# Hand-written orders in a two-layer encoder kernel: first norm, x updates, last norm, third gate operand, and the place of the Fourier constants

## Chip, cores and metric

The kernel runs on one core of a Trainium2 chip. The metric is the device time of one execution in microseconds (us). An execution was also profiled; its span goes from the first to the last instruction of the program.

## What is computed

The input x is 512 tokens by 1024 channels in float32. Two layers of

```
x += 1/2 * SwiGLU(RMSNorm(x))                       # FFN 1
h  = RMSNorm(x)
x += W_o( sigmoid(ga) * NA(h) W_na + sigmoid(gf) * FNet(h) W_f )   # mixer; ga, gf are projections of h plus a bias
x += 1/2 * SwiGLU(RMSNorm(x))                       # FFN 2
```

and a last RMSNorm with a gain. NA is attention over a neighbourhood in an 8 x 64 grid of tokens with a learned bias by relative position; FNet is the real part of a 2-D Fourier transform over positions and the channels of a group. The inner width of an FFN is 2816.

## The kernel before

**Precision and products.** Every float32 operand is split into a high part (a copy on ACT, rounded to the format that PE takes) and a low part (operand minus high part, on DVE); line 285 is the helper, lines 287 and 288 its two instructions. A product is three matmuls (lines 281 to 283): high x high, high x low, low x high. Large products go through a seven-product scheme of Strassen's kind: of the four quarters of a weight and of an activation, sums and differences are made, and products 1 to 7 are added with signs. The weights for it arrive as quarters ("raw", 512 KB) through SP's queue (line 150); some differences are made by an accumulating load on POOL's queue (line 152, line 179), others by an add on DVE (line 170). `Item.prep` (line 164) splits one piece into `whi` (line 172 where it is negated, else 287) and `wlo` (173 or 288); three buffers hold each.

**Order.** The weights form one stream (`ws`): `ws.next()` hands out the next piece and first prepares two pieces further, and each preparation asks for loads up to eight pieces further (FETCH, line 33). A scheduler places the instructions of each engine by priority, which is the place in the program text except under `tc.high_priority()`; where the text says `tc.manual_schedule`, the engines named keep the order of the text. Engines run their instructions strictly in the order so made, each with its waits. PE is TensorE, DVE VectorE, ACT ScalarE, POOL GpSimd, SP the engine that issues most loads.

**First norm.** x comes twice at the start: transposed (`xt`, scaled and split at once in `given`, line 330) and by tokens (`x`, loaded at line 1251 behind eight weight pieces). The 1/rms of a token is applied late: `norm.rstd` (line 389) sums the squares (ACT with an accumulator, line 323, two per block of 128 tokens) and forms 1/sqrt by an integer start and three Newton steps, some 15 tiny operations on DVE (lines 299 to 304, 395 to 408). For the first norm it runs in the middle of the first products; `plain_out` (line 540) then needs it for the first 256 columns of the FFN: a tanh on ACT (line 545) and two operations on DVE (549, 550) for each block, and the transposes of their result (line 486) are the next work of PE after the third product of the first round.

**Updates in an FFN.** The products of the second matrix are added to x with signs by `update` (line 590, 128x512 each). After the last piece of product 6 three updates of two instructions each follow at once (line 680), then those of products 7, 3 and 4. The next norm's squares and transposes of x (`quad`) stand between them.

**Last norm.** In the last FFN the tokens of the second half are ready first: `finish` (line 718) makes 1/rms for them, one pass of 128x1024 for each block of 128 tokens, and stores them. `begin_block` (706) multiplies half of the channels of the other two blocks by the gain beforehand; `finish_block` (711) takes 1/rms for one block (`inverse`, line 372, a chain of twelve tiny operations under high priority), scales one half of the channels on ACT and the other on DVE, and stores them by ACT's and SP's queues. The last product goes block by block, so that block 0 ends 12 matmuls ahead of block 1.

**Mixer.** `stage_mixer` (line 729) loads the Fourier matrices (four loads of 256 KB on POOL's queue, line 747) and rotation constants (SP, 749) at its start, projects U, forms 1/rms and spreads it over the partitions through memory (`spread`, 410: a store and a broadcast load into `R`, both on POOL's queue), projects V, does the transform over positions (`four_pos`, 832, first user of the constants) and over channels, and attention with its bias (POOL, 893). Then come the gates: `gate_block` runs the seven products in the order 1, 5, 2, 6, 7, 3, 4. Its combined operands are made by hand at lines 1145 to 1152: t1 (for product 5) and t2 (for product 6) with ACT and DVE in the order of the text, and t3 (for product 7) by `third`, called after product 1.

Of the kernel before, what the change touches and what calls it, by code (L numbers as in the profile page):

```python
# [9 lines left out]
F32 = mybir.dt.float32  # L10
# [7 lines left out]
P = 128  # L18
# [74 lines left out]
def encoder_kernel(  # L93
# [213 lines left out]
    class Norm:  # L307


        def __init__(self, idx):  # L310
            self.idx = idx
            self.mix = idx % 3 == 1
            self.ssq = small("ssq")
            self.raw = {}
            self.due = []
            self.h = [None, None]
            self.l = [None, None]
# [54 lines left out]
        def inverse(self, tb):  # L372

            a, b = self.ssq[:, tb : tb + 1], self.ssq[:, 4 + tb : 5 + tb]
            e, f = small("e", 1), small("ef", 1)
            with tc.high_priority():
                V.tensor_scalar(e, a, 1.0 / D, EPS, ALU.mult, ALU.add)
                V.tensor_scalar(f, e, -0.5, None, ALU.mult)
                ms, mh, r, t = small("ms", 1), small("mh", 1), small("r", 1), small("rt", 1)
                V.tensor_scalar(ms, b, 1.0 / D, e, ALU.mult, ALU.add)  # L380
                V.tensor_scalar(mh, b, -0.5 / D, f, ALU.mult, ALU.add)
                V.tensor_single_scalar(t.bitcast(I32), ms.bitcast(I32), 1, ALU.logical_shift_right)
                V.tensor_scalar(r.bitcast(I32), t.bitcast(I32), -1.0, float(0x5F3759DF), ALU.mult, ALU.add)
                for _ in range(3):
                    V.tensor_scalar(t, r, r, mh, ALU.mult, ALU.mult)
                    V.tensor_scalar(r, t, 1.5, r, ALU.add, ALU.mult)
            return r

        def rstd(self, js=(0, 1)):
# [3 lines left out]
            ms = small("ms", n)  # L393
            with tc.high_priority():
# [75 lines left out]
    def stage_ffn(norm, nxt, late):  # L470
# [62 lines left out]
        late_at = []  # L533
        if not norm.idx:
            for i in range(2):
                for j in range(2):
                    norm.squares(i, j)
            norm.rstd()

        def plain_out():  # L540
# [69 lines left out]

        for jb in range(NB):
            f0 = 2 + 4 * jb
            pa = pair("A")
            product(pa, acts[1], K4, True)
            s1 = snap(pa)
            if jb:
                settle_at()
            pb = pair("B")
            product(pb, acts[5], K4, True)
            sb = snap(pb)  # L620
            if jb == 0 and norm.idx == 0:
                plain_out()
            else:
                settle_at()
            product(pa, acts[6], K4, False, again=True)
# [20 lines left out]
        for i, (m, c, _) in enumerate(steps):  # L646
# [16 lines left out]
            if not late:  # L663
                if i == 6:
                    nxt.quad(0, 0)
                elif m == 4 and c == 0:
                    nxt.quad(1, 1)
                    nxt.quad(0, 1)
            if c < 2:
                continue  # L670
            if m == 1:
                update(ps[1], 0, 0, -1)
            elif m == 2:
                update(ps[2], 0, 0, 1)
                nxt.squares(0, 0)
            elif m == 5:
                update(ps[5], 0, 1, 1)
                update(ps[5], 1, 1, -1)
            elif m == 6:
                for q in ((1, 1, 1), (0, 1, -1), (1, 0, 1)):  # L680
                    update(ps[1], *q)
            elif m == 7:
                update(ps[7], 1, 1, 1)
                nxt.squares(1, 1)
            elif m == 3:
                update(ps[3], 0, 1, 1)
                nxt.squares(0, 1)
                if late:
                    make(i + 3)
                    finish(nxt, 1)  # L690
                    for b in range(2):
                        begin_block(b)
            elif late:
                for b in range(2):
# [10 lines left out]

    def begin_block(tb):

        ob[tb] = slot(F32, "o", (D,))
        V.tensor_tensor(ob[tb][:, 0:T], x[:, tb, 0:T], gf[0][:, 0:T], ALU.mult)

    def finish_block(norm, tb):
        r, o_ = norm.inverse(tb), ob[tb]
        S.activation(o_[:, 0:T], o_[:, 0:T], AF.Copy, scale=r)
        S.dma_start(out=out[:, tb, 0:T], in_=o_[:, 0:T])
        V.scalar_tensor_tensor(o_[:, T:D], x[:, tb, T:D], r, gf[0][:, T:D], ALU.mult, ALU.mult)
        nc.sync.dma_start(out=out[:, tb, T:D], in_=o_[:, T:D])

# [11 lines left out]
    def stage_mixer(l, norm, nxt):  # L729
# [11 lines left out]
        nc.sync.dma_start(out=msk, in_=mask)  # L741
        dfs = [hilo("dft") for _ in range(2)]
        rt = slot(F32, "rot", (2, T))
        rots = [rt[:, 0, :], rt[:, 1, :]]
        for hl in range(2):
            for c in range(2):
                G.dma_start(out=dfs[c][hl], in_=dft[hl, c])
            src = bass.AP(tensor=rot.tensor, offset=rot.offset + hl * T, ap=[[0, P], [1, T]])
            nc.sync.dma_start(out=rots[hl], in_=src)

# [19 lines left out]
        def proj_U():  # L770
# [27 lines left out]
            norm.rstd()  # L798
            norm.spread(R)
            outs = []  # L800
            for c in range(2):
# [336 lines left out]
        def minus(p, q, s):  # L1138
            t, u = slot(F32, s), slot(F32, s)
            for z, d in enumerate((t, u)):  # L1140
                V.tensor_tensor(d, p[z], q[z], ALU.subtract)
            V.tensor_tensor(t, t, u, ALU.add)
            return t

        with tc.manual_schedule(engines={mybir.EngineType.DVE, mybir.EngineType.Activation}):
            ws.prep(ws.pos + 3)
            t12 = minus(B[0, 0], B[0, 1], "t1")
            acts[5] = parts(t12, "t1")
            for z in B[1, 1]:
                V.tensor_tensor(t12, t12, z, ALU.add)  # L1150
# [5 lines left out]
        def third():  # L1156
            acts[7] = parts(minus(B[0, 1], B[1, 1], "t3"), "t3")

# [4 lines left out]

        ga0 = gate_block(0, bias, acts, {1: third, 6: fourth})

# [76 lines left out]
    with tc.manual_schedule(engines={mybir.EngineType.SP}):  # L1242
        for kts in ((0,), (1,), (2, 3), (4, 5), (6, 7)):
# [147 lines left out]
```

## Time and profile before

| | us |
|---|---|
| three runs | 1950.65, 1950.5, 1947.32 (median 1950.5) |
| profiled execution | 1946.62 |
| its span | 1944.8 |
| PE busy | 1913.3 (98%) |
| DVE busy | 1617.2 (83%) |
| ACT busy | 1121.6 (58%) |
| mean granted TensorE clock | 0.997 |

Busy time is the union of an engine's instructions. Matmuls are pipelined: a 128x512 one is shown with about 0.39 us and the next starts after 0.227. A line of a timeline gives the start, the duration, the engine, the line of the kernel, the operation, out<-in, the form, how many were merged, and in brackets the idle time of the engine before it with what ended that. `LDWEIGHTS` and matmuls of PE are separate rows. "PEclk" is the granted clock as a share of the full one.

### The profile page before, as it was taken

The page shows a single profiled execution, that of the slowest core. Times are in us where ns is not written, and L with a number is a line of the kernel's source. Part 1 is how long each engine was busy: PE and PEld are TensorE (multiplying, and loading weights), DVE is VectorE, ACT ScalarE, POOL GpSimd, SP SyncE. Part 2 cuts the span into 40 slices and gives each one's busy share as a digit, 9 for nine tenths or more (in the row PEclk, how much of TensorE's full clock was granted, in tenths as well). Part 3 has the DMA queues.
Part 4 walks back from the last instruction along what each step waited for, and adds up shares of the span by engine and source line. Part 5 has one row for each costly group of instructions (what it writes and reads, how often), then busy time and mean ns, then how long its engine had stood idle before and what let it go on. Part 6 is the DMA issues. An engine that isn't in the chain of part 4 may idle for free.

```text
span 1944.8 us, 24572 instructions
## 1 busy us (share of the span) xinstructions
PE 1913.3 (98%) x8997; PEld 1582.6 (81%) x8997; DVE 1617.2 (83%) x1949; ACT 1121.6 (58%) x1596; POOL 198.7 (10%) x242
## 2 busy tenths in 40 slices
PE   8999999999999999999999999999999999999997
PEld 6888887888788888888788888878887888888885
DVE  8777899598789877889977878995978888787898
ACT  6555665346556655566655556653565566555654
POOL 0001011200111010001000100102111110000010
PEclk9999999999999999999999999999999999999999
DMA  9677499221997477649747765983029974766593
GB/s 314 165 195 201 151 248 325 80 72 44 256 232 204 131 190 207 177 156 261 233 139 198 198 174 164 276 277 102 31 87 255 240 185 131 210 181 173 173 281 125
DMA packets 105417, 361.83 MB, mean 186 GB/s; under 512 B 11984, under 2 KB 14160, under 8 KB 105296
## 3 DMA queue, kind: packets, MB, share of 16 engines
q1 hardware_dynamic: 77856, 266.37, 39.0%
q0 software_dynamic: 27008, 93.34, 26.2%
q8 instruction: 71, 1.16, 0.2%
q10 hardware_dynamic: 432, 0.55, 0.1%
q14 instruction: 50, 0.41, 0.1%
HBM read 354.97 MB, written 2.10 MB: 184 GB/s over the span
## 4 chain that ended last, share of the span: by engine, by line
PE 78%; DVE 13%; DMA 4%; issue 3%; ACT 2%; SPq 0%; POOL 0%; ACTq 0%; DVEq 0%; POOLq 0%
PE A L281 8%; PE A L283 8%; PE A L282 8%; PE B L283 4%; PE B L281 4%; PE o L282 4%; PE B L282 4%; PE o L283 4%; PE o L281 4%; PE ps L282 4%; PE ps L281 4%; PE ps L283 4%; DVE wlo L288 4%; DMA raw<-in_wst_dram 3%; PE C L282 2%
## 5 line engine op out<-in xcount | busy, mean ns | idle before, releaser
L288 DVE TENSOR_TENSOR wlo<-raw,whi 128x1024 fp32r<-128x1024 f32 (+1 forms) x522 | 620.2, 1194 | 258.4 <-ACT whi L287 256.1
L287 ACT ACTIVATE whi<-raw 128x1024 fp32r<-128x1024 f32 (+1 forms) x522 | 540.2, 1038 | 508.3 <-PE A L283 131.3
L152 POOL DMA_DIRECT2D raw<-in_wst_dram x152 | 131.2, 874 | 1341.2 <-DMA raw<-in_wst_dram 542.6
L170 DVE TENSOR_TENSOR raw<-raw,raw 128x1024 f32<-128x1024 f32 (+1 forms) x128 | 150.9, 1189 | 2.4
L282 PE MATMUL A<-wlo,xh 128*128 128x512 f32 x384 | 149.6, 390 | 1.4 <-DVE wlo L173 1.4
L283 PE MATMUL A<-whi,xl 128*128 128x512 f32 x384 | 149.5, 389 | 0.0
L281 PE MATMUL A<-whi,xh 128*128 128x512 f32 x384 | 149.3, 390 | 0.0
L172 ACT ACTIVATE whi<-raw 128x1024 fp32r<-128x1024 f32 x76 | 78.9, 1039 | 71.4 <-PE B L283 33.2
L173 DVE SCALAR_TENSOR_TENSOR wlo<-raw,whi 128x1024 fp32r<-128x1024 f32 x76 | 89.9, 1194 | 13.4 <-ACT whi L172 13.4
L282 PEld LDWEIGHTS A<-wlo,xh 128*128 128x128 f32 x384 | 72.1, 188 | 17.3 <-DVE wlo L173 2.3
L281 PEld LDWEIGHTS A<-whi,xh 128*128 128x128 f32 x384 | 71.9, 188 | 15.5 <-ACT whi L172 0.7
L283 PEld LDWEIGHTS A<-whi,xl 128*128 128x128 f32 x384 | 72.1, 188 | 14.9
L463 ACT ACTIVATE sn<-A 128x512 f32<-128x512 f32 x96 | 56.8, 599 | 42.6 <-PE A L283 42.6
L281 PE MATMUL A<-whi,t3h 128*128 128x512 f32 x192 | 75.0, 391 | 3.2 <-ACT sn L463 2.4
L282 PE MATMUL B<-wlo,t1h 128*128 128x512 f32 x192 | 75.1, 391 | 1.0 <-DVE wlo L288 1.0
L281 PE MATMUL B<-whi,t1h 128*128 128x512 f32 x192 | 75.9, 397 | 0.0
L282 PE MATMUL C<-wlo,xh 128*128 128x512 f32 x192 | 75.6, 394 | 0.0
L281 PE MATMUL C<-whi,xh 128*128 128x512 f32 x192 | 75.4, 393 | 0.0
L283 PE MATMUL C<-whi,xl 128*128 128x512 f32 x192 | 75.2, 392 | 0.0
L281 PE MATMUL A<-whi,t2h 128*128 128x512 f32 x192 | 75.1, 391 | 0.0
L282 PE MATMUL A<-wlo,t2h 128*128 128x512 f32 x192 | 74.8, 390 | 0.1
L283 PE MATMUL B<-whi,t1l 128*128 128x512 f32 x192 | 74.8, 390 | 0.0
(347 smaller groups left out, 4919.1 us busy)
## 6 DMA issues: line engine op xcount, KB each, us to landing
raw<-in_wst_dram SPq DMA_DIRECT2D x463, 512.0 KB
raw<-in_wst_dram POOLq DMA_DIRECT2D x168, 512.0 KB, 7.5
raw<-in_wst_dram SPq DMA_DIRECT2D x30, 256.0 KB
vs<-v SPq DMA_DIRECT2D x12, 256.0 KB
bw<-in_rpb_dram SPq DMA_DIRECT2D x32, 68.0 KB
x<-in_xin_dram SPq DMA_DIRECT2D x4, 512.0 KB
raw<-in_wst_dram POOLq DMA_DIRECT2D x8, 256.0 KB, 8.4
dft<-in_dft_dram POOLq DMA_DIRECT2D x8, 256.0 KB, 8.3
```

The costliest lines, as they stand in the source:

```text
L152: G.dma_start(out=self.t, in_=wst[GRAN_AT[self.plus]][:, 0 : self.n], accum_op=ALU.add)
L170: V.tensor_tensor(t, t, self.add.t, ALU.add)
L172: S.activation(hi, t, AF.Copy, scale=-1.0)
L173: V.scalar_tensor_tensor(lo, t, -1.0, hi.bitcast(F32), ALU.mult, ALU.subtract)
L281: PE.matmul(ps, lh, rh, start=start, stop=False, skip_group_check=again)
L282: PE.matmul(ps, lh, rl, start=False, stop=False, skip_group_check=again)
L283: PE.matmul(ps, ll, rh, start=False, stop=stop, skip_group_check=again)
L287: S.activation(hi, src, AF.Copy)
L288: V.tensor_tensor(lo, src, hi.bitcast(F32), ALU.subtract)
L463: S.activation(t[:, b, :], ps[b], AF.Copy)
```

## The change

Five places are edited; no arithmetic is added or dropped.

- **Start.** Six instead of eight weight pieces are asked for ahead of x; the other two follow behind x and the identity. The squares, `rstd`, the first two products with their snapshots (copies of PSUM to SBUF) and `plain_out` of the first norm stand in one `manual_schedule` block for DVE and ACT.
- **Updates of x.** Of the three updates after product 6, the second goes behind the updates and squares of product 7, the third behind those of product 3.
- **Last norm.** `finish` moves behind product 4's first piece, followed by the gain multiplication for the first half of the channels of both other blocks; `rstd` of the last norm loses its high priority. The ends of both blocks are one `manual_schedule` block for DVE and ACT, in which `inverse` is a generator whose steps are placed one by one; three of four quarter results are scaled on ACT, one on DVE.
- **Third gate operand.** Its two subtractions and its sum are placed between the operations of t1 and t2 in the manual block; its high copy stands ahead of the preparation of the second weight piece of the gate's first product.
- **Fourier constants.** The loads of the matrices, and those of the rotation (now on POOL's queue as well), are issued behind the two DMAs of `spread`.

```diff
+                with tc.manual_schedule(engines={mybir.EngineType.DVE, mybir.EngineType.Activation}):
+                    for i in range(2):
+                        for j in range(2):
+                            norm.squares(i, j)
+                    norm.rstd()
+                    pa, pb, s1, sb = two(False)
+                    plain_out()
...
+            if m == 4 and c == 0 and late:
+                finish(nxt, 1)
+                for b in range(2):
+                    gained(b, 0)
...
             elif m == 6:
-                for q in ((1, 1, 1), (0, 1, -1), (1, 0, 1)):
-                    update(ps[1], *q)
+                update(ps[1], 1, 1, 1)
             elif m == 7:
                 update(ps[7], 1, 1, 1)
                 nxt.squares(1, 1)
+                update(ps[1], 0, 1, -1)
             elif m == 3:
                 update(ps[3], 0, 1, 1)
                 nxt.squares(0, 1)
+                update(ps[1], 1, 0, 1)
...
             elif late:
-                for b in range(2):
-                    update(ps[7], 1, 0, 1, (b,))
-                    nxt.squares(1, 0, (b,))
-                    finish_block(nxt, b)
+                with tc.manual_schedule(engines={mybir.EngineType.DVE, mybir.EngineType.Activation}):
+                    chain = [nxt.inverse(b) for b in range(2)]
+                    for z in chain:
+                        next(z)
+                    update(ps[7], 1, 0, 1, (0,))
+                    nxt.squares(1, 0, (0,))
+                    gained(0, 1)
+                    next(chain[0])
+                    update(ps[7], 1, 0, 1, (1,))
+                    nxt.squares(1, 0, (1,))
+                    for _ in chain[0]:
+                        pass
+                    scaled(nxt, 0, 0)
+                    scaled(nxt, 0, 1)
+                    for _ in chain[1]:
+                        pass
+                    scaled(nxt, 1, 0)
+                    whole(nxt, 1, 1)
...
         with tc.manual_schedule(engines={mybir.EngineType.DVE, mybir.EngineType.Activation}):
             ws.prep(ws.pos + 3)
-            t12 = minus(B[0, 0], B[0, 1], "t1")
-            acts[5] = parts(t12, "t1")
+            *_, (t12, _) = minus(B[0, 0], B[0, 1], "t1")
+            h1 = high(t12, "t1")
+            third = minus(B[0, 1], B[1, 1], "t3")
+            next(third)
+            acts[5] = low(h1, t12, "t1")
             for z in B[1, 1]:
                 V.tensor_tensor(t12, t12, z, ALU.add)
-            acts[6] = parts(t12, "t2")
-            w = [ws.next(), ws.next()]
+            h2 = high(t12, "t2")
+            next(third)
+            acts[6] = low(h2, t12, "t2")
+            t3, _ = next(third)
+            w = [ws.next()]
+            h3 = high(t3, "t3")
+            w.append(ws.next())
+            acts[7] = low(h3, t3, "t3")
...
-        ga0 = gate_block(0, bias, acts, {1: third, 6: fourth})
+        ga0 = gate_block(0, bias, acts, {6: fourth})
...
-        ws.fetch(FETCH)
+        ws.fetch(6)
         for tb in range(TB):
             nc.sync.dma_start(out=x[:, tb, :], in_=xin[:, tb, :])
         nc.sync.dma_start(out=idents, in_=ident_in)
+        ws.fetch(FETCH)
```

`gained` is one multiplication of half the channels of a block by the gain on DVE, `scaled` a scaling by 1/rms on ACT with its store on ACT's queue, `whole` both multiplications in one operation on DVE with its store on SP's queue, `two` the first two products of a round. Within `inverse` the two operations that need only the first half of the squares come first and a `yield` follows; further ones stand after each Newton step.

More of the change, by code (lines that the diff above doesn't have):

```diff
@@ L1 @@
-from contextlib import ExitStack
+from contextlib import ExitStack, nullcontext
 import numpy as np
@@ L313, in __init__ @@
             self.ssq = small("ssq")
+            self.inv = {}
             self.raw = {}
@@ L533, in stage_ffn @@
         late_at = []
[L534 to L538, printed above, removed]
         def plain_out():
@@ L609, in make, with two @@
                 made[i] = hl(f(), c, f"c{m}")
-        for jb in range(NB):
-            f0 = 2 + 4 * jb
+        def two(settle):
             pa = pair("A")
@@ L619, in stage_ffn @@
             product(pb, acts[5], K4, True)
-            sb = snap(pb)
-            if jb == 0 and norm.idx == 0:
-                plain_out()
-            else:
-                settle_at()
+            return pa, pb, s1, snap(pb)
+        for jb in range(NB):
+            f0 = 2 + 4 * jb
+            if jb or norm.idx:
+                pa, pb, s1, sb = two(jb)
+                settle_at()
+            else:
+                with tc.manual_schedule(engines={mybir.EngineType.DVE, mybir.EngineType.Activation}):
[5 more added lines that the diff above has]
+                    plain_out()
             product(pa, acts[6], K4, False, again=True)
@@ L704, in encoder_kernel, with half, gained, scaled @@
     ob = {}
[L706 to L716, printed above, removed]
+    def half(tb, i):
+        c = slice(i * T, (i + 1) * T)
+        return ob[tb][:, c], x[:, tb, c], gf[0][:, c], out[:, tb, c]
+    def gained(tb, i):
+        if tb not in ob:
+            ob[tb] = slot(F32, "o", (D,))
+        o_, v, g, _ = half(tb, i)
+        V.tensor_tensor(o_, v, g, ALU.mult)
+    def scaled(norm, tb, i):
+        o_, _, _, to = half(tb, i)
+        S.activation(o_, o_, AF.Copy, scale=norm.inv[tb])
+        S.dma_start(out=to, in_=o_)
+    def whole(norm, tb, i):
+        o_, v, g, to = half(tb, i)
+        V.scalar_tensor_tensor(o_, v, norm.inv[tb], g, ALU.mult, ALU.mult)
+        nc.sync.dma_start(out=to, in_=o_)
     def finish(norm, j):
@@ L741, in stage_mixer, with constants @@
         nc.sync.dma_start(out=msk, in_=mask)
[L742 to L749, printed above, removed]
+        dfs, rots = [], []
+        def constants():
+            for _ in range(2):
+                dfs.append(hilo("dft"))
+            rt = slot(F32, "rot", (2, T))
+            for hl in range(2):
+                for c in range(2):
+                    tc.keep_in_program_order(G.dma_start(out=dfs[c][hl], in_=dft[hl, c]))
+                src = bass.AP(tensor=rot.tensor, offset=rot.offset + hl * T, ap=[[0, P], [1, T]])
+                rots.append(rt[:, hl, :])
+                tc.keep_in_program_order(G.dma_start(out=rots[hl], in_=src))
         def wide():
@@ L799, in proj_U @@
             norm.spread(R)
+            constants()
             outs = []
```

53 lines of the change are left out of this document (29 added, 24 removed).

## The prediction

> **What bounds it now.** I read the busy shares first, then every idle stretch of the matrix engine in the timeline, and then, at each, the engines that feed it.
>
> ```profile
> PE 1913.3 (98%) x8997; PEld 1582.6 (81%) x8997; DVE 1617.2 (83%) x1949; ACT 1121.6 (58%) x1596; POOL 198.7 (10%) x242
> ```
>
> PE is the bound: a 128x512 matmul follows the next every 0.227 us, and summed over the run the starts are only some 30 us later than these steps. So an order on DVE or ACT pays only where PE waits for it, or after PE's last matmul. The timeline of PE shows few such places that the edits touch: the start, the third operand of the gates (twice), one seam between layers, and the end.
>
> ```profile
> 47.47 0.89 PE L486 MATMUL tr<-ident,th 128*128 128x128 f32 x4 [2.11 <-issue]
> 49.22 0.50 PE L281 MATMUL A<-whi,t3h 128*128 128x512 f32 x1 [0.86 <-DVE th L550]
> ...
> 509.19 0.50 PE L282 MATMUL A<-wlo,xh 128*128 128x512 f32 x1 [0.71 <-DVE wlo L173]
> ...
> 529.86 0.50 PE L281 MATMUL A<-whi,t3h 128*128 128x512 f32 x1 [0.97 <-ACT sn L463]
> ...
> 950.40 0.73 PE L281 MATMUL o<-whi,c3h 128*128 128x512 f32 x2 [1.29 <-ACT whi L287]
> 952.37 0.50 PE L282 MATMUL o<-wlo,c3h 128*128 128x512 f32 x1 [1.24 <-DVE wlo L288]
> ```
>
> The bracket is the idle time; from start to start a wait costs about 0.16 more, since a matmul's last 0.16 us overlap the next (2.27 and 1.02 in the first two rows). A wait can also cost clock. In the windows view (span, PE busy, then other columns, PEclk third from the end):
>
> ```profile
> 46.62:50.04 3.42, 1.67 (x9) 1.00 0.53 162
> 50.04:53.45 3.41, 3.41 (x12) 0.50 0.53 141
> 947.74:951.15 3.41, 2.11 (x9) 1.00 0.28 94
> 951.15:954.56 3.41, 2.19 (x10) 1.00 0.91 288
> 949.00:952.41 3.41, 0.89 (x4) 1.00 0.63 197
> ```
>
> After a stretch with 1.67 us busy of 3.41 the clock is halved for the next 3.41 us: matmuls then start 0.43 us apart and some 1.7 us are lost. The last row has only 0.89 busy, yet no drop follows: the clock seems to be judged in fixed stretches of 3.41 us, into which the two waits at 950 happened to fall apart, 2.11 and 2.19 busy. That phase need not be the same in another run.
>
> **The change, part by part.** Steps: a 128x1024 operation on DVE follows the next every 1.14 us, a copy on ACT every 0.96, an update of x (128x512) every 0.60, a square 0.61; a tiny operation in the 1/rms chain that needs the one before it, 0.20.
>
> First norm. The loads of x go ahead of two weight pieces on SP's queue. There a 512 KB load takes 1.28 us (the spacing of SP's issues), so x is whole some 2.5 us earlier and the two pieces come four loads and the identity, 5.4 us, later; POOL's two accumulating loads into them follow, issued at 24.9 and 26.2 instead of 19.49 and 20.77. In the first 62 us such a load takes 5.6 to 11.2 us to land, so the first high part can be copied at 31 to 34 instead of 30.2, the second at 35 to 37.5 instead of 34.2. On DVE the chain of 15 tiny operations now stands whole ahead of all weight work: the last five squares follow the copy of xh on ACT (28.0 + 1.07 + 5 x 0.61, near 32.2), the chain ends at 35.1, the first low part at 36.3. PE needs it at 34.4: a new wait of 1.8. The adds and low parts behind it on DVE run as late, and PE waits 0.8 and 0.6 more in the third product. What it buys is that the tanh no longer waits for a chain spread over 11 us (34.35 to 45.48): but the th operations now stand between four weight operations of 1.14, and PE's transposes still wait 1.6 and the next product 1.0. Together 5.8, against 3.3 plus 1.7 of clock before. The old drop may or may not come again; I take +0.8, with bounds -0.4 (loads land at 5.6, no drop) and +2.5 (a drop as before).
>
> Updates of x. Of six updates in a row (line 680), four move behind later products.
>
> ```profile
> 944.37 3.67 DVE L590 SCALAR_TENSOR_TENSOR x<-o,x 128x512 f32<-128x512 f32 x6
> 947.96 2.35 DVE L170 TENSOR_TENSOR raw<-raw,raw 128x1024 f32<-128x1024 f32 x2
> ```
>
> The weight adds behind them, for which ACT and so PE wait at 950, come 4 x 0.60 = 2.4 earlier. Of 1.45 and 1.41 (start to start) some 0.6 stays: -2.3; bounds -2.9 (all gone) and -1.4 (only the first). The moved updates go where DVE works 1 to 2 us ahead of PE. At the same place of the two FFNs ahead of the mixers PE does not wait for the burst: -0.1 each.
>
> Fourier constants. The four loads land 7.1 to 8.5 us after issue; behind R (issued 362.56) they are there by about 374, and PE reads them first at 389.6, DVE the rotation at 391.2. POOL's adds of the bias move back by six issues of 0.57 = 3.4 us, from 374.4 to 378, and are read from 417.7. R itself gains nothing: POOL waits there for the row (7.0), not for the constants. SP loses two issues of 0.4. Cost 0, hidden by the V projection; without that cover it would be the lateness one for one. Bounds -0.5 and +0.5.
>
> Third gate combination. ACT and DVE of before, in the hand-written block:
>
> ```profile
> 505.68 1.06 ACT L287 ACTIVATE t2h<-t 128x1024 fp32r<-128x1024 f32 x1 [3.81 <-DVE t L1150]
> 506.65 1.05 ACT L172 ACTIVATE whi<-raw 128x1024 fp32r<-128x1024 f32 x1
> ...
> 506.77 1.23 DVE L288 TENSOR_TENSOR t2l<-t,t2h 128x1024 fp32r<-128x1024 f32 x1 [1.13 <-ACT t2h L287]
> 507.92 1.22 DVE L173 SCALAR_TENSOR_TENSOR wlo<-raw,whi 128x1024 fp32r<-128x1024 f32 x1
> ```
>
> The whi at 506.65 is the second weight piece of the first gate product; PE asks for it at 507.7. After the change its copy stands on ACT behind t3h, and t3h needs the sum of t3, which DVE makes only after t2l (the two subtractions fill its idle 1.19 and 1.13 us). So: t3 done 509.1, t3h to 510.2, whi 510.15 to 511.2, PE goes on 3.5 late. Queued behind it on ACT are six more copies that PE and DVE want. On DVE two subtractions for the fourth operand now also precede wlo, which comes at 511.5 to 512.7: 0.8 more. What goes: the two waits of before (0.87 and 0.67 start to start) and part of that at 529.86 (1.14; 1.55 in the second layer), where 0.5 to 1.1 stays because the snapshot copy of A sits in the same ACT queue. 4.8 to 5.4 against 2.7 and 3.1: about +2.2 per gate. Beyond that, 3.4 us idle lie over at most two judged stretches, so one has at most 1.72 busy, and the 0.8 adds to it: like the row with 1.67. A half clock costs up to 1.7; part of it runs while PE would wait anyway, so +0.9. Per gate +3.1, bounds +1.0 (waits half as long, no drop) and +3.9; twice, +6.2.
>
> The Trainium skill, "TensorE: Matmul & The Clock Gate", Part 1, has the same 3413 ns window, but wants a whole idle one before the clock halves. The row with 1.67 us busy speaks against that; by the rule the gates would lose no clock and the sum would be 1.8 lower.
>
> Last norm. Before, from PE's last matmul:
>
> ```profile
> 1935.56 0.69 DVE L590 SCALAR_TENSOR_TENSOR x<-o,x 128x512 f32<-128x512 f32 x1 [0.23 <-PE o L283]
> ...
> 1940.10 0.75 DVE L715 SCALAR_TENSOR_TENSOR o<-x,r,gf 128x512 f32<-128x512 f32 x1
> ```
>
> Then 4.0 us pass until the last store has landed. After, the chain for the first half of the tokens is no longer begun early: it stands behind c4's weight work, and two of the moved updates (1.2) are in front of it, so DVE is some 0.9 later with the first update of x of this step. And the second update, for which PE is done, is queued behind one multiplication by the gain (0.6) and six tiny operations (1.3) that themselves wait for the square on ACT (0.73): it runs about 2.7 later. After it come its square, four and six tiny operations (2.4) and the scaling 0.75. Saved: the two chains no longer share DVE (1.2). Sum +1.9, and +0.3 for later low parts at PE's wait of 1.60 at 1924.76; bounds +0.5 and +3.
>
> Sum: +0.8 -2.3 -0.2 +0 +6.2 +2.2 = +6.7, on the profiled execution's own 1946.6 (span 1944.8, 1.8 around it): 1953.3. The median of the runs is 1950.5, 3.9 above; two of three lie 3.4 to 4.0 above it, which would be two more halved stretches in another phase. The pair of waits at 950 is one candidate, and it goes; the gates lose clock in nearly every phase. So I add only half, 1.9: **1955**.
>
> **Rivals.** First, no clock is lost at the gates: 1953.3 - 1.8 + 1.9 = 1953, chance 0.15. For: the pair at 950 cost none. Against: the row with 1.67. The rule of the Trainium skill named above would have this case.
>
> Second, the start gives back all its 5.0, if the accumulating loads land fast and the transposes find their th ready: 1955 - 5.8 = 1949, chance 0.12. Against: seven DVE operations of 1.14 stand between chain and last th.
>
> Third, the other side: the gates are not slower. One thing sets the price, the lead of ACT and DVE over PE at the second weight piece: now 0.05 us (its copy is done at 507.70, PE goes on at 507.75). With 3.5 us more lead, if other edits let the two engines come to the block earlier than PE, the 6.2 vanish and the waits at 529.86 and 1493.99 go too (-1.2 each): 1955 - 8.6 = 1946, chance 0.12. For: DVE idles 1.19 and 1.13 us in that block. Against: the block starts with attention's last rows, which no edit moves. It ends just about 0.2% faster, and more so with a good start.
>
> The edits do take effect: the instruction order of the built kernel shows each of them.
>
> Forecast 0.55 (1952 to 1961), the rest 0.06 to either side. Within 0.2% (3.9 us, about what a measurement of this kernel can tell from none) are 1946.6 to 1954.4: the first two rivals and the lower edge of the forecast, 0.34; slower 0.56; faster 0.10. Range 1947.5 to 1961.
>
> **What would show it.** Right: a PE idle of 3 us or more at the first gate product of both layers, ended by ACT whi, with PEclk 0.50 soon after; no pair of waits near 950; a PE wait near 35 ended by DVE wlo; 11 us or more from PE's last matmul to the end. Wrong: gates with 1 us or less, a start without waits, or an end of 9.3 or less.

## The result, and the profile after

The changed kernel takes 1954.5 us (median of 14 runs, 1952.8 to 1958.0) beside 1950.6 for the kernel before on the same chip (14 runs, 1946.5 to 1953.2). The ratio is 1.0025, 95% interval 1.0017 to 1.0033: slower by 3 to 6 us; forecast was 1955. The profiled execution took 1953.9 (span 1952.1), 7.3 more than that of before.

The first line of the page of the changed kernel, busy time by engine:

```profile
PE 1915.1 (98%) x8997; PEld 1584.9 (81%) x8997; DVE 1619.2 (83%) x1949; ACT 1123.5 (58%) x1597; POOL 201.7 (10%) x246
```

Nothing shows here: the same shares, and but for one instruction more on ACT and four on POOL the same counts. The timeline of PE in the changed kernel, at the places shown of before:

```profile
36.39 0.50 PE L282 MATMUL B<-wlo,t1h 128*128 128x512 f32 x1 [0.92 <-DVE wlo L288]
...
50.64 0.55 PE L488 MATMUL tr<-ident,th 128*128 128x128 f32 x3 [1.26 <-DVE th L546]
...
512.37 1.22 PE L281 MATMUL A<-whi,xh 128*128 128x512 f32 x2 [3.47 <-ACT whi L172]
...
955.74 0.50 PE L282 MATMUL o<-wlo,c3h 128*128 128x512 f32 x1 [1.01 <-DVE wlo L288]
...
1930.16 0.50 PE L282 MATMUL o<-wlo,c4h 128*128 128x512 f32 x1 [2.21 <-DVE wlo L288]
```

The number in brackets is PE's idle time. It is the forecast's picture: many waits of 0.3 to 1.3 at the start instead of two, one wait of 3.47 at the first gate product (3.48 in the second layer), no wait for t3h near 530, one of two waits left at 950, and a longer wait for the last low part. ACT at the gate, in the changed kernel:

```profile
506.83 1.06 ACT L1187 ACTIVATE t2h<-t 128x1024 fp32r<-128x1024 f32 x1 [3.87 <-DVE t L1203]
510.32 1.06 ACT L1187 ACTIVATE t3h<-t 128x1024 fp32r<-128x1024 f32 x1 [2.43 <-DVE t L1182]
511.28 1.04 ACT L172 ACTIVATE whi<-raw 128x1024 fp32r<-128x1024 f32 x1
```

Before, `whi` stood directly behind `t2h`, at 506.65. Now ACT idles 2.43 us for the sum of t3 while the next weight piece is ready. The clock there, in three stretches of 3.41 us (span, busy time of PE, PEld, DVE, ACT and POOL, then PEclk, DMA share and GB/s):

```profile
508.55:511.96 3.41, 0.35 (x2) 0.00 (x0) 3.38 (x4) 1.64 (x2) 0.85 (x1) 1.00 1.00 191
511.96:515.37 3.41, 3.00 (x7) 2.01 (x8) 3.41 (x4) 3.41 (x6) 0.00 (x0) 0.50 1.04 191
515.37:518.78 3.41, 3.41 (x10) 2.67 (x9) 3.00 (x3) 2.46 (x5) 1.70 (x2) 0.50 0.67 160
```

PEclk falls to 0.50 as forecast, here for two stretches (the next has 1.00), in the second layer for one. DVE at the end of the changed kernel:

```profile
1937.21 2.48 DVE L757 SCALAR_TENSOR_TENSOR o<-x,r,gf 128x1024 f32<-128x1024 f32 x2
1939.61 1.29 DVE L737 TENSOR_TENSOR o<-x,gf 128x512 f32<-128x512 f32 x2
1940.81 0.69 DVE L586 SCALAR_TENSOR_TENSOR x<-o,x 128x512 f32<-128x512 f32 x1
1941.53 0.69 DVE L737 TENSOR_TENSOR o<-x,gf 128x512 f32<-128x512 f32 x1
...
1943.41 0.68 DVE L586 SCALAR_TENSOR_TENSOR x<-o,x 128x512 f32<-128x512 f32 x1
...
1947.29 0.75 DVE L747 SCALAR_TENSOR_TENSOR o<-x,r,gf 128x512 f32<-128x512 f32 x1
```

PE's last matmul starts at 1940.50, the span ends at 1952.1: a tail of 11.6, before 9.7 (1935.13 to 1944.84).

### The profile page after: what moved, and what is told of

Same layout as the page of the kernel before. It is cut to its first block, busy times and chain, and to the rows that moved or that the text cites. A ratio compares the mean times of both kernels' runs of the same rounds, so it can differ in the third digit from the quotient of the medians.

```text
span 1952.1 us, 24577 instructions
## 1 busy us (share of the span) xinstructions
PE 1915.1 (98%) x8997; PEld 1584.9 (81%) x8997; DVE 1619.2 (83%) x1949; ACT 1123.5 (58%) x1597; POOL 201.7 (10%) x246
## 4 chain that ended last, share of the span: by engine, by line
PE 79%; DVE 12%; DMA 3%; issue 3%; ACT 2%; ACTq 0%; SPq 0%; POOL 0%; DVEq 0%; POOLq 0%
PE A L282 8%; PE A L283 8%; PE A L281 8%; PE o L282 5%; PE o L283 5%; PE o L281 4%; PE B L281 4%; PE B L282 4%; PE B L283 4%; PE ps L282 4%; PE ps L283 4%; PE ps L281 4%; DMA raw<-in_wst_dram 3%; DVE wlo L288 3%; PE C L283 2%
## 5 line engine op out<-in xcount | busy, mean ns | idle before, releaser
L170 DVE TENSOR_TENSOR raw<-raw,raw 128x1024 f32<-128x1024 f32 (+1 forms) x128 | 151.1, 1190 | 2.4
L283 PE MATMUL A<-whi,t2l 128*128 128x512 f32 x192 | 74.8, 389 | 0.0
```

The costliest lines, as they stand in the source:

```text
L170: V.tensor_tensor(t, t, self.add.t, ALU.add)
L283: PE.matmul(ps, ll, rh, start=False, stop=stop, skip_group_check=again)
```

## The experiments

Single times of one kernel lie 1 to 11 us apart. Where the halved stretches fall is a part of that and not all: the fastest and the slowest run of fill13 (1948.8 and 1959.5) were granted 0.998 and 0.997 of the clock. So two things are read of each kernel: its time as a ratio to the kernel before on the same chip, and the **excess** of PE from its own trace of one execution, the time from matmul start to matmul start beyond the usual step (0.227 for 128x512), summed over a part of the span. Half clock is in it. "Tail" is from the start of the last matmul to the end of the span. All in us.

| kernel | ratio to before (95%) | excess 30–65 | 500–570 | 905–970 | 1455–1530 | tail |
|---|---|---|---|---|---|---|
| before | 1 | 5.4 | 3.3 | 3.9 | 4.1 | 9.7 |
| changed | 1.0025 (1.0017–1.0033) | 6.6 | 6.8 | 2.3 | 7.6 | 11.6 |
| u_gate | 1.0004 (0.9995–1.0012) | 8.1 | 4.3 | 1.6 | 4.8 | 11.6 |
| m_gate | 1.0010 (1.0001–1.0019) | 8.1 | 4.8 | 1.6 | 4.1 | 11.6 |
| u_last | 1.0026 (1.0016–1.0036) | 8.3 | 5.8 | 1.6 | 6.4 | 10.0 |
| u_start | 1.0017 (1.0008–1.0027) | 6.3 | 5.4 | 1.6 | 6.5 | 11.6 |
| u_upd | 1.0046 (1.0033–1.0058) | 8.1 | 6.2 | 6.1 | 6.8 | 11.6 |
| fill13 | 1.0018 (1.0008–1.0028) | 6.9 | 4.4 + 2.95 | 1.6 | 3.9 + 2.95 | 11.6 |
| u_order | 0.9997 (0.9988–1.0006) | 2.6 | 6.2 | 1.6 | 7.4 | 11.6 |
| u_load | 1.0016 (1.0008–1.0025) | 5.9 | 6.2 | 1.6 | 7.2 | 11.6 |
| u_const | 1.0021 (1.0011–1.0031) | 7.0 | 6.8 | 1.9 | 6.7 | 11.3 |
| swap | one run, 1955.3 | 8.6 | 6.9 | 1.6 | 6.3 | 11.4 |
| early | one run, 1953.2 | 8.1 | 6.6 | 1.6 | 6.0 | 10.6 |
| best | 0.9943 (0.9931–0.9956) | 2.7 | 2.3 | 1.6 | 2.9 | 9.8 |

A difference of two ratios in us is their difference times 1950; with intervals of about ±0.0009 each it is known to some ±2.5 us. The 2.95 of fill13 are its added matmuls. The columns leave out PE's wait near 1927; behind it the clock halved in u_gate, u_last, u_start and u_const (excess from 1915 on 4.1 to 4.3, in the others 2.0 to 2.7).

### The gate edit undone: u_gate

```
+            acts[6] = parts(t12, "t2")
+            w = [ws.next(), ws.next()]
...
+        def third():
+            acts[7] = parts(minus(B[0, 1], B[1, 1], "t3"), "t3")
```

> The changed kernel with the third gate operand put back (its subtractions, sum and copies again behind product 1), all else as changed. Theory A, the terms of the forecast: the loss sits at the gates, so the idle of 3.47 us at the first gate product goes in both layers, the waits of before (0.71 and 0.97 idle in the first layer) come back, no half clock follows, and the time is some 6 us below the changed kernel's 1954.5, near 1948.5. Rival B, only waits count and the clock is no part of it: the waits sum to 4.61 and 4.71 in the changed kernel and 2.68 and 3.09 before, so 3.5 us less, near 1951. Rival C, the loss sits at the start or in the tail: within 1 us of 1954.5.

Measured 4.1 below the changed kernel (1.0004 against 1.0025). The idle of 3.47 is gone in both layers, no half clock follows, the waits of before are back (0.71 and 0.52, then 1.43 at t3h). The excess falls by 2.5 and 2.8 from the changed kernel's, by 1.1 to 1.7 from those of u_start and u_last. So a loss sits at the gates, and rival C falls. Its size lies nearer to the waits alone (3.5) than to the forecast (6), but ±2.3 holds both.

### Only the copy moved: m_gate

```
-            w = [ws.next()]
+            w = [ws.next(), ws.next()]
             h3 = high(t3, "t3")
-            w.append(ws.next())
```

> The changed kernel with one line moved: t3's subtractions and sum stay early, but its high copy on ACT stands behind the preparation of the second weight piece. Theory A names the place of the copy in ACT's queue as the cause: the idle of 3.47 us falls to 1 us or less in both layers, there is no half clock at 508 to 520 and 1474 to 1484, the wait for t3h near 530 and 1494 stays away, and the time is at or a little below that of the kernel with the gate edit undone, 1946 to 1949. Rival: the subtractions on DVE ahead of the weight's low part are what costs; then 2 to 3 us of idle stay at the first gate product, ended by DVE, and the time is 1951 to 1954.

Measured 2.9 below the changed kernel (±2.5), not told apart from u_gate; its median, 1951.3, lies in the rival's range, so it is the trace that decides. The longest wait of PE in m_gate's timeline at the first gate product:

```profile
514.07 0.50 PE L282 MATMUL A<-wlo,xh 128*128 128x512 f32 x1 [0.90 <-DVE wlo L173]
```

The wait for `whi` falls from 3.47 to none at this piece: the copy's place was the cause. What stays, 0.90 ended by DVE, is the rival's small part: t3's sum (1.22) stands ahead of the low part on DVE. The wait for t3h, which theory A had away, is 0.38 at 532 in the first layer and 1.18 at 1495 in the second.

### Last norm undone: u_last

```
-            if m == 4 and c == 0 and late:
-                finish(nxt, 1)
...
+                for b in range(2):
+                    update(ps[7], 1, 0, 1, (b,))
+                    nxt.squares(1, 0, (b,))
+                    finish_block(nxt, b)
```

> The changed kernel with the last norm put back to the order of before, the x updates stay moved. Theory A: from the start of the last matmul to the end of the span 9.7 instead of 11.6 us, and PE's wait near 1927 within 0.4 of 2.37; in all 1.9 to 2.2 us less than the changed kernel, near 1952.5. Rival: the moved updates, not the new order of the end, make DVE late; then the tail stays at 11 or more and the time at 1954.

The tail is 9.95, 1.67 shorter; PE's wait ahead of it is 2.40 against 2.21 idle. So the new order at the end costs 1.5 locally. The times do not show it (1.0026 against 1.0025): the effect is below their ±2.5. In this profile a halved stretch from 1930.8 on, which the changed kernel's lacks, takes about as much.

### Start undone: u_start

```
-                with tc.manual_schedule(engines={mybir.EngineType.DVE, mybir.EngineType.Activation}):
...
-        ws.fetch(6)
+        ws.fetch(FETCH)
```

> The changed kernel with the start put back (eight pieces ahead of x, no hand-written order for the first norm). Theory A: the waits of 2.3 and 1.0 near 47 to 50 come back in place of seven waits that sum to 5.7, a half clock may follow them; the time is within 1.5 us of the changed kernel, between 1953 and 1955.5. Rival C, the start carries the loss: 3 us or more below 1954.5.

Measured 1.6 below the changed kernel (±2.4): theory A's 1.5 fits, and rival C's 3 is not shut out by the time. The waits came back as theory A said (2.29 and 0.81 from start to start at 45 and 48). The excess is 6.3, with two halved stretches in it; in the kernels with the changed start it was 6.6 to 8.6 (with one halved stretch where over 8). What looks like a small effect is the sum of two, as the next ones show.

### The hand-written order undone, the loads kept: u_order

```
+        if not norm.idx:
+            for i in range(2):
+                for j in range(2):
+                    norm.squares(i, j)
+            norm.rstd()
...
-                with tc.manual_schedule(engines={mybir.EngineType.DVE, mybir.EngineType.Activation}):
```

> The changed kernel without the hand-written order of the first norm (squares, 1/rms and the first FFN tile placed by priority as before); the loads of x stay ahead of two weight pieces. Theory A2, formed after the four runs so far: the hand-written order is what costs at the start, since it holds the low parts of the second product behind the whole 1/rms chain, while earlier loads of x gain; then the wait at the transposes near 47 to 50 goes without new ones of more than 1.3 us in sum over the second product, and the time is 3 to 5 us below the changed kernel's. Rival: the two weight pieces that come later are what costs; then waits of 2 us or more stay at 34 to 40, and the time is within 1.5 us of the changed kernel's.

Measured 5.5 below the changed kernel (±2.4), and the excess at the start is 2.6, the lowest so far. ACT and then DVE in the changed kernel:

```profile
37.23 1.06 ACT L287 ACTIVATE whi<-raw 128x1024 fp32r<-128x1024 f32 x1 [2.54 <-DMA raw<-in_wst_dram]
...
40.73 1.06 ACT L287 ACTIVATE whi<-raw 128x1024 fp32r<-128x1024 f32 x1 [1.46 <-DVE raw L170]
```

```profile
38.33 1.23 DVE L288 TENSOR_TENSOR wlo<-raw,whi 128x1024 fp32r<-128x1024 f32 x1 [1.99 <-ACT whi L287]
39.47 1.22 DVE L170 TENSOR_TENSOR raw<-raw,raw 128x1024 f32<-128x1024 f32 x1
41.82 1.23 DVE L288 TENSOR_TENSOR wlo<-raw,whi 128x1024 fp32r<-128x1024 f32 x1 [1.13 <-ACT whi L287]
```

and DVE in u_order:

```profile
37.08 1.22 DVE L170 TENSOR_TENSOR raw<-raw,raw 128x1024 f32<-128x1024 f32 x1
38.73 2.36 DVE L288 TENSOR_TENSOR wlo<-raw,whi 128x1024 fp32r<-128x1024 f32 x2 [0.44 <-ACT whi L287]
```

In the order of the text, the weight add L170, which u_order can begin at 37.08, stands behind a low part that waits 1.99 for a late load. By priority the add fills that gap, 2.4 earlier, and the last th operation begins at 48.23 instead of 53.82. No wait follows at 47 to 52. The Newton steps of 1/rms end at about the same time in both (35.3 and 34.9), and though the two tiny operations behind them end 2.0 later in u_order (37.2 against 35.2), its first tanh begins 4.2 earlier (41.97 against 46.22): the compact chain bought nothing.

### The loads undone, the order kept: u_load

```
-        ws.fetch(6)
+        ws.fetch(FETCH)
```

> The changed kernel with eight weight pieces ahead of x again; the hand-written order of the first norm stays. It is the fourth corner of the start (both edits, neither, and the loads alone are measured). Theory A2, the hand-written order costs and the earlier loads gain, each by itself: the chain of 1/rms now ends some 2.5 us later (x is whole that much later), the low parts behind it too, and the time is 1 to 4 us above the changed kernel's, with a wait of 2.5 us or more near 35 ended by DVE wlo. Rival, the two edits cost only together, because POOL's later accumulating loads meet the hand-written order: then the waits near 34 to 40 shrink to 1 us in sum and the time is 2 us or more below the changed kernel's.

Measured 1.8 below the changed kernel, which the interval (±2.3) does not tell from none; theory A2's rise of 1 to 4 is not there. PE waits at the second product's low part, ended by DVE, about as theory A2 said (2.5):

```profile
37.84 0.50 PE L282 MATMUL B<-wlo,t1h 128*128 128x512 f32 x1 [2.31 <-DVE wlo L288]
```

A halved stretch follows at 39.32. The next wait is 1.20 at 51.83, and there is none in between: POOL issues its accumulating loads at 19.75 and 21.02 instead of 24.73 and 27.15, and the weight pieces are there in time for the hand-written order. The four corners of the start, as ratios: both edits 1.0025, neither 1.0017, order alone 1.0016, loads alone 0.9997. The earlier loads of x gain 3.9 with the order made by priority, and with the one written out they gain nothing (1.8 lost, not told from none). The order costs 5.5 with x early and nothing with x late (1.0016 against 1.0017). So the two edits are not additive, and theory A2 was wrong on "each by itself". The rival had it: the order costs only together with POOL's later accumulating loads (the late load above is one of them). Only the wait that the rival expected to go did not.

### x updates undone: u_upd

```
-                update(ps[1], 1, 1, 1)
+                for q in ((1, 1, 1), (0, 1, -1), (1, 0, 1)):
+                    update(ps[1], *q)
...
-                update(ps[1], 0, 1, -1)
...
-                update(ps[1], 1, 0, 1)
```

> The changed kernel with the x updates put back in one row of six after product 6. Theory A: the two waits near 950 come back (1.45 and 1.41 from start to start before, against one of 0.57 to 1.17 in the four changed kernels profiled so far), so the time is 1.7 to 2.3 us above the changed kernel's. PE's wait near 1927 falls from 2.4 towards 1.8. Rival: the moved updates only shift the lateness of DVE to other places; then the sum of PE's waits stays and the time is within 0.5 us of the changed kernel's.

Measured 4.1 above the changed kernel (±2.9), so the rival falls. PE's wait near 1927 falls to 1.54 from start to start. Both waits at 950 are back (1.77 and 1.24 idle), and in this execution they fell into one stretch: 1.24 busy of 3.41, half clock behind it, an excess of 6.1 against 1.6. Without the halved stretch (1.7) that is 2.8 lost. In the 11 other kernels with the updates moved the excess is 1.6 to 1.9, in the changed kernel's profile 2.3. So the updates gain 1.6 to 2.3 of the 3.9 there; 2.3 was forecast.

### The idle at the gates filled: fill13

```
+            def idle():
+                pw = bank()
+                for _ in range(13):
+                    PE.matmul(pw, hx[0][:, 0, 0:P], xs[0][0], start=True, stop=True)
...
+                    product(pa, acts[1], K4, True, hook=None if i else idle)
```

> The changed kernel with 13 matmuls of 128x512 more, into a bank of PSUM that nobody reads, behind the first weight piece of the gates' first product in both layers. They take 13 x 0.227 = 2.95 us and stand in the idle of 3.47, so the copy on ACT ends the wait at the same time as without them. Theory A, the half clock after the gates comes from this idle and costs time: no granted clock of 0.50 at 508 to 520 and 1474 to 1484, and 2 to 4 us less than the changed kernel (one or two halved stretches in each layer, part of them beside waits). Rival, the half clock costs nothing since PE waits there anyway: the clock is full and the time within 0.7 us of the changed kernel's.

A window of fill13 over the same work, and one wait of its second layer:

```profile
513.41:516.82 3.41, 3.15 (x13) 1.99 (x12) 3.41 (x4) 3.41 (x7) 0.00 (x0) 1.00 0.91 223
```

```profile
1499.39 0.50 PE L281 MATMUL A<-whi,t3h 128*128 128x512 f32 x1 [1.93 <-ACT sn L465]
```

The clock is full here and in the windows beside it, in both layers, so the idle is what halves it. Yet the part takes no less: 4.4 + 2.95 = 7.35 in the first layer (changed kernel 6.8, others with the gate edit 5.4 to 6.9), 3.9 + 2.95 = 6.85 in the second (6.0 to 7.6). What the full clock gives, PE spends waiting: 1.93 for t3h in the second layer, and low parts at 541 to 557 in the first. The time is 1.4 below the changed kernel's, ±2.5, which settles nothing by itself. By this one trace, in both layers, the rival is right: ACT and DVE set the pace behind the gap, and a half clock beside it is nearly free.

### The Fourier constants undone: u_const

```
+        dfs = [hilo("dft") for _ in range(2)]
...
-            constants()
```

> The changed kernel with the loads of the Fourier constants back at the mixer's start (four on POOL's queue, two of the rotation on SP's). Theory A: nothing in the mixers waits for them in either place; PE's waits between 350 and 500 stay 1.4 in sum (1.3 to 2.2 in the profiles so far), and the time is within 1 us of the changed kernel's, by what its measurement can tell. Rival, the six issues on POOL's queue between R and the bias delay the attention: then the waits near 422 to 452 (0.67 and 0.85) shrink by 0.3 or more each and the time falls by 1 to 2 us.

Measured 0.8 below, ±2.5: no difference told. PE's waits at 422 and 452 are 0.67 and 0.85 as before. Nothing waits for the constants in either place.

### The end: swap and early

```
                     update(ps[7], 1, 0, 1, (0,))
                     nxt.squares(1, 0, (0,))
+                    update(ps[7], 1, 0, 1, (1,))
+                    nxt.squares(1, 0, (1,))
                     gained(0, 1)
                     next(chain[0])
-                    update(ps[7], 1, 0, 1, (1,))
-                    nxt.squares(1, 0, (1,))
```

> The changed kernel with one move in its last block: the second update of x and its square stand directly behind the first update and its square, ahead of the multiplication by the gain and the six tiny operations. Theory A, as the forecast put it (the second update runs late behind these, and all that follows with it): the second update comes 1.5 to 2 us earlier and the time from the start of the last matmul to the end falls from 11.6 to 10 or less. Rival, it is the amount of work that DVE still has after PE's end, not its order, that sets the end: the tail stays within 0.4 of 11.6.

The tail is 11.4, as the rival has it. DVE in swap:

```profile
1942.40 1.28 DVE L586 SCALAR_TENSOR_TENSOR x<-o,x 128x512 f32<-128x512 f32 x2
...
1944.20 0.21 DVE L382 TENSOR_SCALAR ms<-ssq,e 128x1 f32<-128x1 f32 x1
...
1946.38 0.20 DVE L382 TENSOR_SCALAR ms<-ssq,e 128x1 f32<-128x1 f32 x1
...
1948.67 0.75 DVE L747 SCALAR_TENSOR_TENSOR o<-x,r,gf 128x512 f32<-128x512 f32 x1
```

The second update now follows the first at once, but the chain of block 0 takes 1944.20 to 1946.4 and that of block 1 as long again, one behind the other. From the end of the second update to the start of the last operation of DVE lie 5.0 us; in u_last, where the two chains interleave, 3.85.

For early, `finish` and `gained` stand behind product 3 again:

```
-            if m == 4 and c == 0 and late:
-                finish(nxt, 1)
-                for b in range(2):
-                    gained(b, 0)
...
                     make(i + 3)
+                    finish(nxt, 1)
+                    for b in range(2):
+                        gained(b, 0)
```

> The changed kernel with the norm of the second half of the tokens, and the multiplication by the gain for the first half of the channels, back at their place behind product 3, and with high priority for its 1/rms chain; the last block stays hand-written. Theory B, DVE's backlog before the last block makes the tail: the last block begins some 1 us earlier and the tail is 10.3 to 10.9. Theory A, the order inside the last block makes it: the tail stays at 11.4 or more. If DVE is full in both places, what the tail gains PE's wait near 1927 loses, which is 2.37 in the changed kernel and 2.56 with all of the last norm put back.

The tail is 10.6, as theory B has it: DVE reaches the first update 0.68 before PE's last matmul starts (1940.12 and 1940.80), in the changed kernel 0.31 after it. PE's wait ahead of it is 2.42 instead of 2.21. So of the 1.67 between 11.62 and 9.95 some 1.0 is DVE coming late; the other 0.67 goes with the block's own order, and the chains in a row are the only longer piece that the rows show. No run has the written block with its chains interleaved, so this last part is a reading.

### The parts that gain, together: best

```
+            w = [ws.next(), ws.next()]
             t3, _ = next(third)
-            w = [ws.next()]
             h3 = high(t3, "t3")
-            w.append(ws.next())
```

This is the kernel before with the moved updates, the earlier loads of x, and the gate block with these lines (shown against the changed kernel).

> The kernel before with three parts of the change, one of them mended: the moved x updates; the loads of x ahead of two weight pieces (without the hand-written order of the first norm); and the third gate operand with both subtractions early in DVE's idle places, but its sum, high copy and low part behind both weight pieces of the first gate product. Theory A2: against the kernel before, 2 less at 950, 1 to 1.5 less at each gate (no wait for t3h near 529 and 1493, the waits of 0.87 and 0.67 smaller), 2 to 5 less at the start with its half clock: 1941 to 1945 where the kernel before takes 1950. Rival, the gains are given back later, since DVE is 83% busy: within 2 us of the kernel before.

Measured 1938.3 (5 runs, 1936.4 to 1940.2) beside 1948.8: 0.9943, 95% interval 0.9931 to 0.9956, 11 us faster than before and 16 than the changed kernel. The excess is lower at each place, by 2.7 at the start, 1.0 and 1.2 at the gates, 2.3 at 950, and no stretch has half clock before PE's last matmuls. The wait for `whi` at the first gate product is gone, one for t3h is left, 0.61 at 526 and 0.89 at 1487, behind the copy of the snapshot on ACT. The four places make 7.2; some is given back, above all at 631 to 639, where PE waits for DVE's updates of x in the first mixer (1.9 of excess, in the kernel before none), and over the whole run the excess falls by 6.5. The rest of the 11 us lies between single runs and medians: the profiled execution of before is 2.2 below its median here, that of best 1.9 above its own; where the other runs differ was not seen.

## Why the prediction came out, step by step

The total was right, 1955 for 1954.5, with its sign. Between the two profiled executions the difference is 7.3, and the terms gave 6.7. The 7.3 can be told place by place: the excess of the whole run rises from 30.5 to 35.9, by 1.2 at the start and 3.5 at each of the two gates, while 1.6 go at 950 and 1.2 elsewhere in pieces under 1 us; the tail adds 1.9. The terms were right to different degrees, errors of size offset each other, and the last step to the median was a guess that fitted.

- **Gates, +6.2 forecast.** Place, length (3.5 late, 3.47 idle), engine and the missing wait near 530 were right, and the half clock came. In the changed kernel's own profile the gates take 7.0 more than before; undoing the edit gives 4.1 (±2.3), which holds 6.2 as well. What the runs speak against is the clock's share, +0.9 a layer: fill13 shows the section as long with a full clock. What the forecast called "part of it runs while PE would wait anyway" is nearly all of it. The waits alone, 2 x 2.2 = 4.4 by the forecast and 3.5 as measured, fit the 4.1.
- **Start, +0.8.** The waits were there, eight of them, 5.7 in sum against 5.8 forecast. "The old drop may or may not come again" was the open part: of nine profiles with both start edits, six show a half clock at 52 to 58 (excess 8.1 to 8.6) and three none (6.6 to 7.0), with 5.4 for the kernel before. So +1.2 to +3.2 by excess: a term too small by 0.4 to 2.4. The time, 1.6 (±2.4), does not tell. The mechanism given was only part of it: besides the compact chain it was the order of the text that held a ready weight add behind a late load. By the four corners that order costs nothing where the weight loads are not later.
- **Updates of x, -2.3.** Excess 3.9 before, 1.6 in nearly all profiles: -2.3 as worked out (-1.6 in the changed kernel's own profile); undoing them let a halved stretch in as well, so that their worth can be more.
- **Last norm, +1.9 tail and +0.3.** Tail +1.9 was measured; the wait grew by 0.6, and by u_upd (1.54) and u_last (2.56) that is the moved updates' part. But the inner working failed at one step: the second update "runs about 2.7 later", and with it all that comes after. It does run 2.5 later (0.43 behind the start of the last matmul before, 2.91 after), but the end does not hang on it: swap moves it to the front, and the end stays. "The two chains no longer share DVE (1.2)" was counted as saved, where the rows give the interleaved chains as the faster form (3.85 against 5.0). The late first update held: 0.9 forecast, 0.8 by the rows (1934.64 for a last matmul at 1935.13 before, 1940.81 for 1940.50 after), and the tail gains 1.0 without it (early).
- **Fourier constants, 0.** Held.
- **The step to the median, +1.9.** It was half of the 3.9 by which the profiled execution of before lies below its median, taken for halved stretches in other phases. The profiled execution of the changed kernel lies 0.6 below its own median, so the medians are 3.9 apart where the profiled executions are 7.3; the half came out right without a reason that the runs show.

The rivals: the third (gates not slower) and the second (the start gives back all) did not come, though the earlier loads alone give back half of it: in u_order the start's excess is 2.6 against 5.4. "No clock is lost at the gates" is the one of the three that the runs come nearest to, though not by its mechanism, since the clock does halve. The rule of the Trainium skill, "TensorE: Matmul & The Clock Gate", Part 1, that a whole idle window must pass before the clock halves, is not what the traces show: of the 32 halvings before PE's last matmuls in the 14 profiles, one followed an idle stretch (0.00 us busy), the others stretches with 0.19 to 1.85 us busy. Its free-running window agrees: every halved spell lasted 3.41 or 6.83 us, and within a profile they begin whole multiples of 3.413 us apart.

## What to carry to other kernels

An order written out by hand freezes a guess of when each load lands: one late load then holds all ready work behind it, so write out only the few instructions whose place matters and leave the others to priority. Before a copy is placed ahead of another on an in-order engine, ask which of the two the bound engine wants first, and when the copy's own input is ready; filling idle places with work that is needed much later is good only for the part that is ready there. Edits of one stage are tried in all corners: here two that cost little together were a gain of 4 us and a loss of 5.5 that comes only beside it.

## What the runs showed of the hardware

The stretches that the clock is judged by lie on a fixed grid, in another phase in each execution: in u_start, for example, the halvings before PE's last matmuls begin 136, 418 and 551 times 3.413 us behind the first. Laid on the grid of its profile, every stretch at full clock with 1.43 us or less of PE busy was followed by half clock (23 stretches), and none with 1.88 or more. Between these, nine of 17 were. In the changed kernel one with 1.74 was followed by full clock:

```profile
1928.49:1931.90 3.41, 1.74 (x8) 1.44 (x9) 3.41 (x4) 1.21 (x2) 0.00 (x0) 1.00 0.00 0
```

and in u_order two stretches of 1.52 and 1.56 came one behind the other (1.48 and 1.60 on the grid, which lies 0.04 later), and only the second brought the half clock:

```profile
503.72:507.14 3.42, 1.52 (x7) 0.94 (x5) 3.37 (x4) 0.99 (x2) 1.43 (x2) 1.00 1.08 322
507.14:510.55 3.41, 1.56 (x5) 0.78 (x5) 3.38 (x4) 3.41 (x5) 0.00 (x0) 1.00 1.06 197
510.55:513.96 3.41, 3.41 (x10) 2.64 (x9) 3.41 (x4) 3.38 (x7) 0.96 (x2) 0.51 0.46 161
```

Once halved, a stretch with 3.00 or less busy was followed by another halved one (seven cases, from 2.31 up), one with 3.09 or more was not. The ends of matmuls are modelled, so busy time is an approximation, and what exactly is judged between 1.48 and 1.85 stays open.
